# Four edits to a one-core encoder layer: one exponential per head over both key blocks, rotary tables on VectorE, late queries turned ahead of a round's last block, and an empty stage between load and squares

## The chip, the cores and the metric

The kernel runs on one NeuronCore of one Trainium2 chip, in one launch. A core has five engines with queues of their own: TensorE (PE, its weight loads shown as PEld), VectorE (DVE), ScalarE (ACT), GpSimd (POOL) and SyncE (SP), which here issues every DMA. The metric is the device time of the whole launch in microseconds, as the median of several runs.

## The reference: what is computed

One layer of a bidirectional encoder is applied to two groups of rows with the same weights: the prompt of 512 rows and the sample of 1024 rows, all of width 1024, in 32-bit floating point.

```python
a = _rmsnorm(h, norm_mix_g)
z = a @ w_in                                    # 1024 -> 8 q heads, 2 k, 2 v of 64, and 512 pooling channels
o_attn = _attention(q, k, v, q_norm_g, k_norm_g)  # q/k RMSNorm, 2-D rotary, softmax over all keys
o_pool = _pool_mixer(u, w_pool, pool_scale)       # means over windows of 2, 4, 8, 16, minus u, then 128x128
h = h + jnp.concatenate([o_attn, o_pool], axis=-1) @ w_out
m = _rmsnorm(h, norm_mlp_g)
h = h + jnp.square(jax.nn.relu(m @ w_up)) @ w_down   # 1024 -> 4096 -> 1024
gate = sigmoid(_rmsnorm(h, norm_ple_g) @ w_ple_gate)
h = h + gate * (p_i @ w_ple_proj)
return _rmsnorm(h, final_norm_g)
```

The softmax of a query row runs over 512 keys in the prompt and over 1024 keys in the sample.

## The kernel before

**Precision.** Each 32-bit operand of a large product is split into a high and a low part (`hi` a rounded copy, `lo` what is left), and a product is made of three matmuls (`three`, line 103). So nearly every operand passes two engines before TensorE can use it: a copy on ScalarE and a subtraction on VectorE or GpSimd.

**Order of the work.** The order on TensorE, ScalarE, VectorE and GpSimd is written out by hand: each engine runs its instructions in the order in which the code emits them, and waits for whatever the instruction at its head needs. Only SP's order, that of the DMAs, is found by the planner when the kernel is built. Most tiles in SBUF come from one pool of 49 buffers of the same size (`slot`, line 74); a load can be issued once a buffer is free for it. Two PSUM banks (`tp_ps`, line 84) serve all transposes and some small products in turn; a transpose waits until the bank it gets was read.

**The stages in order.**

1. *Input projection* (lines 1137 to 1183, to about 200 us). The rows are twelve tiles of 128: tiles 0 to 3 the prompt, 4 to 11 the sample. Tiles 0 and 1 run together while the weights arrive, then `mm_k(t, k)` goes tile by tile over eight slices `k`. `evac` (line 260) scales the result out of PSUM, squares the heads and sums them (VectorE, lines 280 and 282); `rstd_of` (line 97) makes the inverse root on GpSimd, an addition and a power (lines 99 and 100). `rotary_steps` (line 290) applies it and the rotary tables on VectorE (lines 292 to 309). One tile later `turn_qk` (line 327) transposes queries and keys into the two transposition banks as `qp` and `kp` and splits them (ScalarE lines 340 and 341, VectorE lines 343 and 344); `turn_u` (line 311) does the same for the pooling channels. The tables `tab` are the products of the gains with cosines and sines (lines 210 to 224); each is 128x512. GpSimd makes them, after a constant of ones (lines 201 to 203).
2. *Attention* (lines 1190 to 1285, to about 552 us). A `Unit` is a tile of 128 queries with one key/value head and its four query heads. The loop over `at` takes one query head per round: `soften` (the exponential of the head before, line 444), `score` (this head's scores and their maximum, line 433), `norm` (line 452), then `turn` and `split` (lines 463 and 470) of one or two key tiles of the unit before, and `weigh` (line 475), their product with the values. A round ends with one or two blocks out of `fill`: pieces of the pooling output or of the output projection (`pool_out`, `heads_out`), which are matmuls that need little from the other engines. In the prompt's rounds an even `at` takes two blocks and an odd one takes one; in the sample's rounds at most one is taken, and from `at` = 62 on only in some rounds. `extras` (line 1197) holds work that is left from the projection: `turn_u` of tile 11 in round 3, `turn_qk` of tile 10 in round 8 and of tile 11 in round 18, and the steps of the last rotary in rounds 6 to 10. It runs after the round's blocks (line 1270). GpSimd and ScalarE also run `chores`, a queue of generators that advance a step at a time, such as the preparation of the MLP's inputs (`make_m`, line 579).
3. *MLP* (from about 575 us). The rows are three chunks of 512. Products are arranged with seven instead of eight block products (`ORDER`, `UP`, `DOWN`); the prepared up-weights of the first chunk are kept in DRAM (`kept_d`) and fetched again for the others (tile `w`), and down-weights (`we`) are loaded and combined for pairs of tiles (`Double`). Between the products, `chores` finish the earlier chunks.
4. *Gate and final norm* (from about 1566 us): lines 1564 to 1630.

**The softmax.** For the sample a head's scores are 128x1024 over two PSUM banks, `S`. `soften` runs two exponentials, one for each block of 512 keys, each with its own accumulated sum; `norm` adds the two sums on VectorE (line 455), takes the reciprocal (line 456) and scales both blocks on GpSimd (line 461). A buffer of probabilities holds one key block of two heads. For the prompt there is one block, one sum and the reciprocal of line 458.

**The gating chore.** `gating(0)` (line 1394) runs during the third chunk's products. For each of four quarters of chunk 0 it loads the finished rows (`load_h` out of `hl_d`), squares them on ScalarE (line 1406) and scales them into the gate's inputs (lines 1357 and 1359), adds the squares on GpSimd (line 1413), and stores the inputs (line 1419). `staged` (line 667) interleaves the quarters: in a round, later stages of earlier quarters come ahead of earlier stages of later ones.

```python
    def staged(items, *stages):
        for t in range(len(items) + len(stages) - 1):
            for s in reversed(range(len(stages))):
                if 0 <= t - s < len(items):
                    yield from stages[s](items[t - s])
```

Of the kernel before, what the change touches and what calls it, by code (L numbers as in the profile page):

```python
# [18 lines left out]
P = 128  # L19
D = 1024  # L20
# [15 lines left out]
def encoder_layer(ctx, tc, xT, xn, xr, pT, w1, w2, w_pool, w_out, w_up, w_down, w_gate, w_proj,  # L36
# [18 lines left out]
    def load(dst, src):  # L55
        ins = sy.dma_start(dst, src).ins
        if last_pe[0] is not None:
            tc.add_manual_dep(ins, last_pe[0].name, NOSYNC, reason="not before its turn")
# [55 lines left out]
    def load_x(t, parts=(slice(0, KD),)):  # L114
        raw = slot([P, KD, P], F32, f"xt{t}")
        for part in parts:
            load(raw[:, part], xT[t][:, part])
        return raw
# [8 lines left out]
    def load_xn(t):  # L127
        nat = slot([P, D], F32, f"xn{t}")
        load(nat, xn[t * P:(t + 1) * P, :])
        return nat  # L130
# [34 lines left out]
    wps = tp_ps("warm")  # L165
    for i in range(8):
        pe.matmul(wps, wz[:, 0:P], wz, start=True, stop=True)
    load(gmix_sb, g_mix)
    head, tail = slice(0, 2), slice(2, KD)
    x0 = load_x(0, (head,))  # L170
# [13 lines left out]
    for k in range(3, KD):  # L184
        if k + 1 < KD:
            raws.append(load_w(k + 1))
        split_w(k, raws[k])
    n0, n1 = load_xn(0), load_xn(1)
    x2, n2 = load_x(2), load_xn(2)
    stat_x(0, n0)  # L190
    stat_x(1, n1)
# [6 lines left out]
    load(gmlp_sb, g_mlp)  # L198
    gfin_sb = const.tile([P, KD], F32, name="gfin_sb")
    load(gfin_sb, g_fin)  # L200
    ones_sb = const.tile([P, P], F32R, name="ones_sb")
    gp.memset(as32(ones_sb), 1.0)
    gp.tensor_scalar(ones_sb, as32(ones_sb), 1.0, 1.0, op0=ALU.mult, op1=ALU.mult)
    psc_sb = const.tile([P, 4], F32, name="psc_sb")
    load(psc_sb, p_scale)
    edge_sb = const.tile([P, 4, 2 * PAD], F32, name="edge_sb")
    load(edge_sb, edge)


    csr = slot([P, 2, 8, 32], F32, "csr")  # L210
    load(csr, cs)
    tab = {}
    for nm, g in (("q", q_g), ("k", k_g)):
        graw = small.tile([P, HD], F32, tag="graw", name=f"g{nm}", bufs=2)
        load(graw, g)
        if nm == "k":
            gp.tensor_scalar(graw, graw, 8.0, None, op0=ALU.mult)
        tb = slot([P, 2, 8, HD], F32, f"tab{nm}")
        for i in range(2):
            gp.tensor_tensor(  # L220
                tb[:, i].rearrange("p a (b c) -> p a b c", b=2),
                graw.rearrange("p (b c) -> p b c", b=2).unsqueeze(1).to_broadcast([P, 8, 2, 32]),
                csr[:, i].unsqueeze(2).to_broadcast([P, 8, 2, 32]), op=ALU.mult)
            tab[nm, i] = tb[:, i]

    def transpose4(dst, src):
        for i in range(4):
# [192 lines left out]
    class Unit:  # L420


        def __init__(self, s, t, g):
            self.s, self.t, self.g = s, t, g
            self.t0, self.n = SEQS[s]
            self.nc = self.n // 4
            self.id = f"{t}_{g}"
            self.sums = small.tile([P, 4, 2], F32, tag="sums", name=f"sums{self.id}", bufs=3)
            self.pr, self.S = {}, {}
            self.o = None  # L430
            self.pt = {}
# [11 lines left out]

        def soften(self, j):
            S, nm = self.S.pop(j)
            for c in range(self.nc):
                if j % 2 == 0:
                    self.pr[j // 2, c] = slot([P, 2, CH], F32, f"pr{self.id}{j}{c}")
                sc.activation(self.pr[j // 2, c][:, j % 2], S[:, c * CH:(c + 1) * CH], AF.Exp, bias=nm,
                              accum_out=self.sums[:, j, c:c + 1])  # L450

        def norm(self, j):
            rr = small.tile([P, 1], F32, tag="rr", name=f"rr{self.id}{j}")
            if self.nc == 2:
                ve.tensor_tensor(rr, self.sums[:, j, 0:1], self.sums[:, j, 1:2], op=ALU.add)
                ve.reciprocal(rr, rr)  # L456
            else:
                ve.reciprocal(rr, self.sums[:, j, 0:1])
            for c in range(self.nc):
                p = self.pr[j // 2, c][:, j % 2]  # L460
                gp.tensor_scalar(p, p, rr, 1.0, op0=ALU.mult, op1=ALU.mult)  # L461

        def turn(self, kt):
            tp = tp_ps(f"tp{self.id}{kt}")
            c, b = kt // 4, kt % 4
            for j in range(4):
                pe.transpose(tp[:, j * P:(j + 1) * P], self.pr[j // 2, c][:, j % 2, b * P:(b + 1) * P], id_sb)
            self.pt[kt] = tp

        def split(self, kt):  # L470
# [196 lines left out]
    def staged(items, *stages):  # L667
        for t in range(len(items) + len(stages) - 1):
            for s in reversed(range(len(stages))):
                if 0 <= t - s < len(items):  # L670
                    yield from stages[s](items[t - s])

    HALVES = (slice(0, CH), slice(CH, D))

# [543 lines left out]
    for at in range(2, 4 * len(units) + 6):  # L1218
# [41 lines left out]

        n = 0 if at < 3 else 2 - at % 2 if at < first_sample else 1
        took = n and bool(fill)
        for _ in range(n):
            if fill and (at < 62 or at % 2 == 0 and (at < 76 or at % 3 or len(fill) > 10) or at >= 96):
                fill.popleft()()
        fill.extend(ready)
        ready.clear()
        lag = fresh
        last = (cur, j) if cur else None
        if at in extras:  # L1270
            extras[at]()
        if at > 3:
            clock[0] += 1
            if products and products[0][0] < clock[0]:
# [119 lines left out]
    def gating(c):  # L1394
# [24 lines left out]
                sy.dma_start(hg_d[a][i], flat(gin[c, a][i]))  # L1419
            return iter(())  # L1420

        yield from staged(range(4), fetch, square, total, keep)
        gp.tensor_tensor(acc[:, 0], acc[:, 0], acc[:, 1], op=ALU.add)
        yield from wait(6)
        yield from spread_g(c, acc)
# [332 lines left out]
```

## Time and profile before

| what | value |
|---|---|
| median of 3 runs | 1769.13 us (1767.67 to 1769.21) |
| the profiled execution's own time | 1772.11 us |
| its span, first to last instruction | 1770.3 us |
| busy: PE, PEld | 1727.3 us, 1574.4 us |
| busy: DVE, ACT, POOL | 1287.1 us, 906.9 us, 1078.4 us |
| mean granted TensorE clock | 0.992 |
| moved by DMA | 391.78 MB, mean 221 GB/s |

Busy time is read per engine against the span; an engine far below it stands for most of the time and costs something only where another waits for it. In the timeline rows a line gives the start in us from the span's start, the length in us, the engine, the line of the kernel, the operation, the tiles written and read, the shape and the count; in brackets stands the idle time before it and what ended that. In rows of waits stand the total in us, the number of waits and the longest. In rows that group a line's instructions stand the count, then shortest, median and longest duration in ns. DMA rows give the count, the size of one and the median time from issue to landing in us.

### The profile page before, as it was taken

To read this page: it belongs to the slowest core of one execution; us is meant where nothing else is said; L and a number is where in the kernel's file an instruction comes from. 1 tells how busy PE (TensorE), PEld (TensorE's weight loads), DVE (VectorE), ACT (ScalarE), POOL (GpSimd) and SP (SyncE) were. 2 spreads that over 40 slices of the span, in tenths; PEclk is the share of its full clock that TensorE was granted. 3 is DMA by queue.
4 is the path that set the end of the run, shared out by engine and by line. 5 is a ranking of instruction groups with operands and counts; after the bars stand their busy time and mean duration, and the time that the engine had idled before them with its cause. 6 is when DMAs were issued, how large, how long until landed. Compare 5 with 4: busy or idle time off the path is not lost. (4 is left out here: it accounts for less than half of the span.)

```text
span 1770.3 us, 31419 instructions
## 1 busy us (share of the span) xinstructions
PE 1727.3 (98%) x11692; PEld 1574.4 (89%) x11692; DVE 1287.1 (73%) x1786; ACT 906.9 (51%) x1730; POOL 1078.4 (61%) x933
## 2 busy tenths in 40 slices
PE   9999999999999999999999999999999999999997
PEld 7788777888778998989989999999999999998897
DVE  5776765878987668777757766777778788675666
ACT  6334454767885646555445444544444445543333
POOL 3474883534765766859645776865678677654431
PEclk9999999999999999999999999999999999999998
DMA  7232544211326887979798969698776889653012
GB/s 253 84 133 106 217 175 179 72 67 42 124 92 256 322 296 274 361 277 357 285 348 324 344 226 334 223 340 331 248 265 233 308 276 349 252 208 114 12 48 96
DMA packets 133608, 391.78 MB, mean 221 GB/s; under 512 B 14160, under 2 KB 26832, under 8 KB 133456
## 3 DMA queue, kind: packets, MB, share of 16 engines
q1 hardware_dynamic: 133456, 389.78, 60.9%
q8 instruction: 92, 1.51, 0.4%
q14 instruction: 60, 0.49, 0.1%
HBM read 275.96 MB, written 113.77 MB: 220 GB/s over the span
## 5 line engine op out<-in xcount | busy, mean ns | idle before, releaser
L49 PE MATMUL pd<-ta,v 128*128 128x256 f32 x2688 | 339.4, 283 | 0.1
L49 PEld LDWEIGHTS pd<-ta,v 128*128 128x128 f32 x2688 | 329.6, 190 | 0.8 <-POOL v L1033 0.3
L1033 POOL TENSOR_TENSOR v<-we,v 128x512 fp32r<-128x512 f32 x128 | 184.4, 1461 | 105.7 <-DVE ta L1053 37.6
L461 POOL TENSOR_SCALAR pr<-pr,rr 128x512 f32<-128x512 f32 x160 | 111.2, 706 | 135.6 <-DVE rr L456 64.0
L49 PE MATMUL pd<-r,wd 128*128 128x512 f32 x768 | 190.5, 397 | 2.0 <-DVE r L950 2.0
L1033 POOL TENSOR_TENSOR v<-vs,v 128x512 fp32r<-128x512 f32 x96 | 128.0, 1354 | 103.6 <-DVE c L1056 37.2
L49 PE MATMUL z<-w,x 128*128 128x512 f32 (+1 forms) x864 | 175.0, 359 | 2.4 <-ACT w L159 1.1
L1053 DVE TENSOR_TENSOR ta<-c,ta 128x512 fp32r<-128x512 f32 x112 | 115.7, 1033 | 84.4 <-ACT ta L1051 77.1
L49 PEld LDWEIGHTS pd<-r,wd 128*128 128x128 f32 x768 | 140.9, 189 | 31.1 <-DVE r L950 2.8
L49 PEld LDWEIGHTS z<-w,x 128*128 128x128 f32 x864 | 142.4, 188 | 29.3 <-ACT w L159 2.8
L844 POOL TENSOR_TENSOR w<-ws,w 128x512 fp32r<-128x512 f32 x72 | 106.2, 1477 | 92.8 <-ACT w L843 88.0
L49 PE MATMUL pq<-mo,w 128*128 128x256 f32 x1152 | 153.2, 282 | 5.4 <-DMA w<-kept_d 4.2
L49 PE MATMUL pz<-mo,w 128*128 128x256 f32 x1152 | 153.6, 283 | 4.0 <-DVE u L980 3.5
L49 PE MATMUL px<-mo,w 128*128 128x256 f32 x1152 | 153.6, 283 | 0.0
L49 PEld LDWEIGHTS pz<-mo,w 128*128 128x128 f32 x1152 | 146.6, 190 | 7.7 <-DVE u L980 4.1
L49 PEld LDWEIGHTS pq<-mo,w 128*128 128x128 f32 x1152 | 143.7, 189 | 6.7 <-DVE H L1084 2.9
L49 PEld LDWEIGHTS px<-mo,w 128*128 128x128 f32 x1152 | 145.6, 191 | 1.4
L49 PE MATMUL pg<-hg,wg 128*128 128x512 f32 (+1 forms) x768 | 141.1, 338 | 0.3 <-DVE hg L1359 0.3
L49 PEld LDWEIGHTS pg<-hg,wg 128*128 128x128 f32 x768 | 119.3, 188 | 17.0 <-DVE hg L1359 0.5
L472 ACT CAST pt<-tp 128x512 fp32r<-128x512 f32 x160 | 87.7, 590 | 90.3 <-PE tp L53 88.6
L473 DVE TENSOR_TENSOR pt<-tp,pt 128x512 fp32r<-128x512 f32 x160 | 104.0, 684 | 31.4 <-ACT pt L472 31.0
L441 DVE TENSOR_REDUCE nm<-S 128x1 f32<-128x1024 f32 (+1 forms) x96 | 100.1, 1043 | 22.9 <-PE S L49 22.4
(252 smaller groups left out, 3562.2 us busy)
## 6 DMA issues: line engine op xcount, KB each, us to landing
w<-kept_d SPq DMA_DIRECT2D x210, 512.0 KB, 5.9
kept_d<-w SPq DMA_DIRECT2D x105, 512.0 KB, 5.2
we<-in_w_down_dram SPq DMA_DIRECT2D x64, 512.0 KB, 7.0
mo_d<-mm SPq DMA_DIRECT2D x84, 256.0 KB, 4.2
mo<-mo_d SPq DMA_DIRECT2D x42, 512.0 KB, 10.1
wur<-in_w_up_dram SPq DMA_DIRECT2D x36, 512.0 KB, 5.8
wdr<-in_w_down_dram SPq DMA_DIRECT2D x32, 512.0 KB, 6.8
h_d<-h SPq DMA_DIRECT2D x16, 512.0 KB, 2.9
```

The lines of the kernel that those rows point to most:

```text
L49: last_pe[0] = nc.tensor.matmul(*a, **k).ins
L441: ve.tensor_reduce(nm, S[:, :nch * CH], axis=AX.X, op=ALU.max, negate=True)
L461: gp.tensor_scalar(p, p, rr, 1.0, op0=ALU.mult, op1=ALU.mult)
L472: sc.copy(self.pt[kt][:, 0], tp)
L473: ve.tensor_tensor(self.pt[kt][:, 1], tp, as32(self.pt[kt][:, 0]), op=ALU.subtract)
L844: gp.tensor_tensor(t[:, 1], x, as32(t[:, 0]), op=ALU.subtract)
L1033: ins = gp.tensor_tensor(lo[:, p], src[:, p], as32(hi[:, p]), op=ALU.subtract).ins
L1053: last_ve[0] = ve.tensor_tensor(t[:, 1], x, as32(t[:, 0]), op=ALU.subtract).ins
```

## The change

The diff has four parts that do not touch each other's lines.

1. *Tables.* The load of the cosines and sines, the loads of the two gains and the four table products move ahead of the loads of tile 2 (`load_x(2)`, `load_xn(2)`) and run on VectorE instead of GpSimd. The constant of ones moves to the start of the kernel, behind the warm-up matmuls, and stays on GpSimd.
2. *Softmax.* A head's probabilities are one buffer of 1024 columns in the sample (in the prompt two heads share one); one exponential and one accumulated sum cover both key blocks, the addition of two sums is gone, and GpSimd scales both blocks in one instruction.
3. *Extras.* They run ahead of the round's last block instead of after it; in a round without blocks they run as before.
4. *Gating.* A stage that yields nothing stands between the load of a quarter and its squares, so that in `staged` each quarter's load is issued one turn earlier against its square.

```diff
+    ones_sb = const.tile([P, P], F32R, name="ones_sb")
+    gp.memset(as32(ones_sb), 1.0)
+    gp.tensor_scalar(ones_sb, as32(ones_sb), 1.0, 1.0, op0=ALU.mult, op1=ALU.mult)
     load(gmix_sb, g_mix)
...
     n0, n1 = load_xn(0), load_xn(1)
+    csr = slot([P, 2, 8, 32], F32, "csr")
+    load(csr, cs)
+    tab = {}
+    for nm, g in (("q", q_g), ("k", k_g)):
+        graw = small.tile([P, HD], F32, tag="graw", name=f"g{nm}", bufs=2)
+        load(graw, g)
+        if nm == "k":
+            ve.tensor_scalar(graw, graw, 8.0, None, op0=ALU.mult)
+        tb = slot([P, 2, 8, HD], F32, f"tab{nm}")
+        for i in range(2):
+            ve.tensor_tensor(
...
     x2, n2 = load_x(2), load_xn(2)
...
-    csr = slot([P, 2, 8, 32], F32, "csr")
...
-            gp.tensor_scalar(graw, graw, 8.0, None, op0=ALU.mult)
...
-            gp.tensor_tensor(
...
-            self.sums = small.tile([P, 4, 2], F32, tag="sums", name=f"sums{self.id}", bufs=3)
+            self.sums = small.tile([P, 4], F32, tag="sums", name=f"sums{self.id}", bufs=3)
...
         def soften(self, j):
             S, nm = self.S.pop(j)
-            for c in range(self.nc):
-                if j % 2 == 0:
-                    self.pr[j // 2, c] = slot([P, 2, CH], F32, f"pr{self.id}{j}{c}")
-                sc.activation(self.pr[j // 2, c][:, j % 2], S[:, c * CH:(c + 1) * CH], AF.Exp, bias=nm,
-                              accum_out=self.sums[:, j, c:c + 1])
+            n = self.nc * CH
+            if j not in self.pr:
+                full = slot([P, D], F32, f"pr{self.id}{j}")
+                for i in range(2 // self.nc):
+                    self.pr[j + i] = full[:, i * n:(i + 1) * n]
+            sc.activation(self.pr[j], S[:, :n], AF.Exp, bias=nm, accum_out=self.sums[:, j:j + 1])
 
         def norm(self, j):
             rr = small.tile([P, 1], F32, tag="rr", name=f"rr{self.id}{j}")
-            if self.nc == 2:
-                ve.tensor_tensor(rr, self.sums[:, j, 0:1], self.sums[:, j, 1:2], op=ALU.add)
-                ve.reciprocal(rr, rr)
-            else:
-                ve.reciprocal(rr, self.sums[:, j, 0:1])
-            for c in range(self.nc):
-                p = self.pr[j // 2, c][:, j % 2]
-                gp.tensor_scalar(p, p, rr, 1.0, op0=ALU.mult, op1=ALU.mult)
+            ve.reciprocal(rr, self.sums[:, j:j + 1])
+            p = self.pr[j]
+            gp.tensor_scalar(p, p, rr, 1.0, op0=ALU.mult, op1=ALU.mult)
...
+    def idle(item):
+        return iter(())
...
-        for _ in range(n):
-            if fill and (at < 62 or at % 2 == 0 and (at < 76 or at % 3 or len(fill) > 10) or at >= 96):
+        for i in range(max(n, 1)):
+            if i == n - 1 or not n:
+                extras.pop(at, lambda: None)()
+            if n and fill and (at < 62 or at % 2 == 0 and (at < 76 or at % 3 or len(fill) > 10) or at >= 96):
                 fill.popleft()()
...
-        if at in extras:
-            extras[at]()
...
-        yield from staged(range(4), fetch, square, total, keep)
+        yield from staged(range(4), fetch, idle, square, total, keep)
```

More of the change, by code (lines that the diff above doesn't have):

```diff
@@ L188, in encoder_layer @@
     n0, n1 = load_xn(0), load_xn(1)
+    csr = slot([P, 2, 8, 32], F32, "csr")
[9 more added lines that the diff above has]
+            ve.tensor_tensor(
+                tb[:, i].rearrange("p a (b c) -> p a b c", b=2),
+                graw.rearrange("p (b c) -> p b c", b=2).unsqueeze(1).to_broadcast([P, 8, 2, 32]),
+                csr[:, i].unsqueeze(2).to_broadcast([P, 8, 2, 32]), op=ALU.mult)
+            tab[nm, i] = tb[:, i]
     x2, n2 = load_x(2), load_xn(2)
@@ L200, in encoder_layer @@
     load(gfin_sb, g_fin)
-    ones_sb = const.tile([P, P], F32R, name="ones_sb")
-    gp.memset(as32(ones_sb), 1.0)
-    gp.tensor_scalar(ones_sb, as32(ones_sb), 1.0, 1.0, op0=ALU.mult, op1=ALU.mult)
     psc_sb = const.tile([P, 4], F32, name="psc_sb")
@@ L207, in encoder_layer @@
     load(edge_sb, edge)
-    csr = slot([P, 2, 8, 32], F32, "csr")
[L211 to L216, printed above, removed]
-            gp.tensor_scalar(graw, graw, 8.0, None, op0=ALU.mult)
[L218 to L224, printed above, removed]
     def transpose4(dst, src):
@@ L445, in soften @@
             S, nm = self.S.pop(j)
-            for c in range(self.nc):
-                if j % 2 == 0:
-                    self.pr[j // 2, c] = slot([P, 2, CH], F32, f"pr{self.id}{j}{c}")
-                sc.activation(self.pr[j // 2, c][:, j % 2], S[:, c * CH:(c + 1) * CH], AF.Exp, bias=nm,
-                              accum_out=self.sums[:, j, c:c + 1])
+            n = self.nc * CH
[4 more added lines that the diff above has]
+            sc.activation(self.pr[j], S[:, :n], AF.Exp, bias=nm, accum_out=self.sums[:, j:j + 1])
         def norm(self, j):
             rr = small.tile([P, 1], F32, tag="rr", name=f"rr{self.id}{j}")
-            if self.nc == 2:
-                ve.tensor_tensor(rr, self.sums[:, j, 0:1], self.sums[:, j, 1:2], op=ALU.add)
-                ve.reciprocal(rr, rr)
-            else:
-                ve.reciprocal(rr, self.sums[:, j, 0:1])
-            for c in range(self.nc):
-                p = self.pr[j // 2, c][:, j % 2]
-                gp.tensor_scalar(p, p, rr, 1.0, op0=ALU.mult, op1=ALU.mult)
+            ve.reciprocal(rr, self.sums[:, j:j + 1])
+            p = self.pr[j]
+            gp.tensor_scalar(p, p, rr, 1.0, op0=ALU.mult, op1=ALU.mult)
         def turn(self, kt):
             tp = tp_ps(f"tp{self.id}{kt}")
-            c, b = kt // 4, kt % 4
             for j in range(4):
-                pe.transpose(tp[:, j * P:(j + 1) * P], self.pr[j // 2, c][:, j % 2, b * P:(b + 1) * P], id_sb)
+                pe.transpose(tp[:, j * P:(j + 1) * P], self.pr[j][:, kt * P:(kt + 1) * P], id_sb)
             self.pt[kt] = tp
```

## The prediction

> **What bounds the kernel now.** I read the page first, then TensorE's own waits, then windows of 20 us and the timeline around each long wait.
>
> ```profile
> PE 1727.3 (98%) x11692; PEld 1574.4 (89%) x11692; DVE 1287.1 (73%) x1786; ACT 906.9 (51%) x1730; POOL 1078.4 (61%) x933
> ```
>
> TensorE is busy 1727.3 us of a span of 1770.3, and none of the edits removes a matmul. What the change can win is therefore only the 43.0 us in which TensorE stands, and what the clock loses behind a stand. The waits of TensorE (what waited, on what; us in total, times, longest) say where that is:
>
> ```profile
> PE pq L49 <- DMA w<-kept_d: 4.2, 3, 2.8
> PE qp L53 <- DVE eb L301: 4.1, 2, 2.5
> PE pz L49 <- DVE u L980: 3.5, 1, 3.5
> PE tp L53 <- DVE qs L343: 3.3, 2, 1.6
> PE o L49 <- DVE pt L473: 3.2, 7, 1.0
> ```
>
> Four of these five belong to the four edits: `qp` waits for the first rotary, which needs statistics that queue behind the tables on POOL; `pz` stands next to the gating loads; `tp` waits for banks that the late queries hold; `o` waits for the split of the turned probabilities in the sample's attention. Two stretches (us; busy us of PE, PEld, DVE, ACT, POOL; granted clock; DMA share) show what surrounds them:
>
> ```profile
> 440.00:560.00 120.00, 115.59 (x676) 91.34 (x676) 106.66 (x194) 100.59 (x239) 81.79 (x101) 1.00 0.34 123
> 1480.00:1500.00 20.00, 16.45 (x119) 16.24 (x118) 14.62 (x17) 8.19 (x13) 14.72 (x11) 0.83 0.86 326
> ```
>
> In the second half of the sample's attention TensorE is idle 120 - 115.59 = 4.4 us while VectorE and ScalarE are 89% and 84% busy: there the other engines set the pace now and then. Around 1490 us a stand of 3.5 us goes with a granted clock of 0.83.
>
> **Part 1: rotary tables on VectorE, ones earlier.**
>
> ```profile
> 22.68 0.33 SPq L56 DMA_DIRECT2D csr<-in_cs_dram  x1
> 32.35 1.23 DVE L125 TENSOR_TENSOR x<-xt,x 128x1024 fp32r<-128x1024 f32 x1 [3.60 <-ACT x L124]
> 33.71 2.54 POOL L220 TENSOR_TENSOR tabq<-gq,csr 128x512 f32<-128x512 f32 x2
> 36.98 0.82 DVE L282 TENSOR_REDUCE hs<-ra 128x10 f32<-128x640 f32 x1
> 37.28 2.54 POOL L220 TENSOR_TENSOR tabk<-gk,csr 128x512 f32<-128x512 f32 x2
> 41.67 1.99 POOL L100 TENSOR_TENSOR hr<-hr,mhalf 128x10 f32<-128x10 f32 x1
> 43.70 0.82 DVE L292 TENSOR_TENSOR ea<-ea,hr 128x640 f32<-128x640 f32 x1 [2.35 <-POOL hr L100]
> 44.55 0.69 DVE L295 TENSOR_TENSOR ra<-ea,tabq 128x512 f32<-128x512 f32 x1
> 46.52 0.41 DVE L301 TENSOR_TENSOR eb<-ra,ea 128x256 f32<-128x256 f32 x1
> 47.08 0.63 PE L53 MATMUL qp<-id_sb,eb 128*128 128x128 f32 x4 [2.49 <-DVE eb L301]
> 54.72 0.63 PE L53 MATMUL qp<-id_sb,eb 128*128 128x128 f32 x4 [1.58 <-DVE eb L301]
> xn<-in_xn_dram SPq DMA_DIRECT2D x12, 512.0 KB, 6.3
> ```
>
> The head sums of tile 0 are ready at 36.98 + 0.82 = 37.80, but POOL's last table ends at 37.28 + 2.54 = 39.82 and the power that VectorE needs only at 43.66. With the tables and the ones gone from POOL the power can follow the sums at once (some 0.4 us for the addition ahead of it), and `hr` is there near 40.2, 3.5 us sooner. VectorE then loses its idle 2.35 before L292, so the rotary ends 2.4 us or more earlier, and TensorE, which reached `qp` at 47.08 - 2.49 = 44.59, no longer waits. The second wait (1.58) follows the same chain one tile later: VectorE starts that rotary about 3 us earlier while TensorE comes 2.49 earlier; I leave 0.2 of it. Gain 2.49 + 1.4 = 3.9 us; bounds 2 and 4.1.
>
> What it adds: four products of 128x512 on VectorE, nearest row L295 with 0.69, so 2.8 us with the scaling of `gk`, 2.9. They stand in VectorE's order just ahead of L125, in whose front it idles 3.60 us: that is the cover. It holds if `csr` lands by 32.35 - 2.9 = 29.4. Its load is now issued ahead of tile 2's two loads instead of behind them, so before 22.68; a load of twice its size in this stage takes 6.3 us, which gives 29.0 at the latest. With the cover gone, L125 slips by what is missing, at most the 2.9. The two gain loads and `csr` pass the loads of tile 2 on SP's queue; 256 KB ahead of a 512 KB load delays that by half of its own time at worst, and only the casts of tile 2 stand behind it on ScalarE, which TensorE needs a tile later. I take nothing for it.
>
> A rule speaks against this part: the Trainium skill (GPSIMD Engine Reference, 8. Key points) says that GpSimd shares its SBUF interfaces with VectorE and contends with VectorE instructions that have two SBUF inputs, which the table products are. By that rule they would be slow only if POOL ran long operations beside them; POOL then has just the small statistics of two tiles, so that the sum is the same by rule and by rows.
>
> **Part 2: late queries ahead of the last block.**
>
> ```profile
> 220.85 3.04 PE L49 MATMUL pp<-yb,wo 128*128 128x512 f32 x12
> 222.94 0.66 DVE L473 TENSOR_TENSOR pt<-tp,pt 128x512 fp32r<-128x512 f32 x1
> 223.73 0.60 PE L53 MATMUL qp<-id_sb,eb 128*128 128x128 f32 x4
> 225.57 1.39 DVE L343 TENSOR_TENSOR qs<-qp,qs 64x512 fp32r<-64x512 f32 x2 [0.95 <-ACT qs L340]
> 227.10 0.63 PE L53 MATMUL tp<-id_sb,pr 128*128 128x128 f32 x4 [1.63 <-DVE qs L343]
> 267.16 0.63 PE L53 MATMUL tp<-id_sb,pr 128*128 128x128 f32 x4 [1.62 <-DVE qs L343]
> ```
>
> Two blocks (12 matmuls) take 223.73 - 220.85 = 2.88 us, one 1.44. Put behind the query's transposes instead of ahead, that block covers 1.44 us of the wait of 1.63. But the transposes need both banks, and the second comes free when L473 ends at 223.60; `qp`, now near 222.3, runs in the free bank, and `kp` waits some 0.7 to 0.9 us for the other. First place: gain 0.7. At the second place I expect 1.3, since there the split stands earlier against the blocks. The same move of `turn_u` in an early round hides some tenths. Together 2.2 us; bounds 0 (banks never free in time) and 3.3 + 0.3. The adds of the last block's output and the store of the queries only change places by one block.
>
> **Part 3: a stage between load and squares.**
>
> ```profile
> 1475.15 0.32 SPq L56 DMA_DIRECT2D h<-hl_d  x1
> 1481.71 1.06 ACT L1406 ACTIVATE sqg<-h 128x1024 f32<-128x1024 f32 x1 [3.35 <-DMA h<-hl_d]
> 1484.59 0.69 DVE L1053 TENSOR_TENSOR ta<-c,ta 128x512 fp32r<-128x512 f32 x1 [3.93 <-POOL sqg L1413]
> 1491.40 2.93 PE L49 MATMUL pz<-mo,w 128*128 128x256 f32 x12 [3.55 <-DVE u L980]
> 1498.19 1.58 PE L49 MATMUL pq<-mo,w 128*128 128x256 f32 x12
> SPq L56 <- POOL H L692: 5.7, 1, 5.7
> ```
>
> The load of the fourth quarter is issued at 1475.15, ScalarE's square stands 3.35 us for it, everything behind that in ScalarE's order (the casts that VectorE's L1053 reads) slips, VectorE idles 3.93, and TensorE stands 3.55 at 1487.85. The empty stage leaves every square where it is in the order and issues each load but the first one item earlier, ahead of the previous item's square and totals and of the stores of `hg`. No instruction is added. The square then runs 3.35 sooner, which takes 3.35 of the 3.55. The clock comes on top: 0.17 x 20 = 3.4 us of work lost in that window, seen as 12 matmuls in 2.93 instead of 1.58; part of the slow stretch lies inside the stand, so I take 2.3. Gain 5.6 us; bounds 0 and 3.55 + 3.4 = 6.9.
>
> The Trainium skill (TensorE: Matmul & The Clock Gate, Part 1) says that the window which decides on half speed is free-running. By that rule the clock's 2.3 belongs to how this stand happened to lie, and other stands that remain may catch or lose such a stretch after every shift; the sum would be 3.35 instead of 5.6 if one is caught anew.
>
> The cost is a buffer of 4 KB held longer, and the loads pass weights on SP's queue. The last row (of the waits of SP's queue from 1440 to 1500 us) is a load that stood 5.7 us until a buffer was released; behind it queue the kept weights `w` and the down weights `we`, which TensorE and POOL wait for.
>
> **Part 4: one exponential per head.**
>
> ```profile
> 446.43 0.71 ACT L449 ACTIVATE pr<-S,nm 128x512 f32<-128x512 f32 x1
> 447.10 0.71 ACT L449 ACTIVATE pr<-S,nm 128x512 f32<-128x512 f32 x1
> 448.50 1.30 POOL L610 TENSOR_TENSOR t<-m,t 128x512 f32<-128x512 f32 x1
> 448.54 1.27 DVE L455 TENSOR_TENSOR rr<-sums 128x1 f32<-128x1 f32 x1
> 450.67 1.25 PE L53 MATMUL tp<-id_sb,pr 128*128 128x128 f32 x8 [0.62 <-DVE pt L473]
> L455 DVE TENSOR_TENSOR rr<-sums x64: 145/151/1271, 317.7 to 551.1; 128x1 f32<-128x1 f32 x64
> L458 DVE RECIPROCAL rr<-sums x32: 147/154/164, 198.7 to 314.5; 128x1 f32<-128x1 f32 x32
> ```
>
> A 128x1024 exponential has no row: between 0.71 (width free) and 1.42 (twice), and the square of that shape took 1.06; with the pointer bias I take 1.12. The second half with its accumulator read costs 447.10 - 446.43 = 0.67 of pitch, the wider one 0.41, so ScalarE wins 0.26 a head, 64 x 0.26 = 17 us. VectorE loses 64 additions of two sums. Their median is 151 ns, but one lasted 1.27 us, and it ended at 449.81, just as POOL's subtraction did (449.80): the addition reads two SBUF operands, and it stood until POOL was done, with the split behind it and the transposes behind that (0.62). The reciprocal that stays never took over 164 ns in the prompt. POOL's scaling is one instruction instead of two, no dearer than both.
>
> None of this is on TensorE; it shows where TensorE waits for the split. Lower bound: 0.2 us less in each of the 7 waits for `o`, 1.4. Upper: the 4.4 idle of the window, and as much again in waits that modelled matmul ends hide, 9. I take 4.5, all of the visible idle: the addition and the exponential both stand ahead of the split. The probabilities of the first four key tiles keep their buffers two rounds longer; each head now takes its buffer only when it starts, so the number in use hardly changes.
>
> **Sum.** 3.9 + 2.2 + 5.6 + 4.5 = 16.2. The profiled execution took 1772.1 us (span 1770.3): 1755.9. It lies 3.0 above the median of 1769.1, so the median comes to 1752.9, said as 1753.
>
> **Rivals.**
>
> *Only the two long stands go.* The sample's attention stays bound by the loop transpose, cast, split, and `kp` pays in part 2 what `tp` wins. For it: most additions take 151 ns. Against: the quoted 0.62 follows a held one. Gain 3.9 + 5.6 = 9.5: 1760.
>
> *Attention gives its upper bound.* VectorE at 89% and ScalarE at 84% both become lighter, and short waits vanish too. 9 instead of 4.5, all else as summed: 1748.
>
> *No net change: the stand at 1488 moves.* The earlier loads of `h` meet a full set of buffers, the queue stands as in the row of 5.7, a kept weight comes late and TensorE stands 2.8 with the clock's loss behind it (2.3), twice; the attention gives its lower bound and part 2 nothing. 3.9 + 5.6 + 1.4 - 2 x 5.1 = 0.7: 1768.
>
> *Slower: the kept weights come late throughout.* SP has one order; when the moved loads and the other buffer pattern push `w` behind its use, each such place costs 2.8 + 2.3 = 5.1, as the worst wait for `kept_d` does now. From four places on (20.4) it outweighs the sum of 16.2: 1773. Against: 210 such loads show three waits today.
>
> **How the numbers follow.** Forecast 0.60, two long stands only 0.18, upper bound in attention 0.09, no net change 0.08, slower 0.05. Its own range is 1749 to 1758, from the bounds of parts 2 and 4. Up to 1746 and 1763 the two neighbours fall inside, with 0.13 outside. What this kernel's measurement can tell from no change is about 0.2%, 3.5 us: faster 0.87, same 0.08, slower 0.05.
>
> **What would show it.** Right: no wait of `qp` for L301 and L292 without idle time; L473 instead of L343 as what `tp` or `kp` waits for near 220 us; no DMA wait ahead of L1406, no wait of `pz` near 1490 and a clock of 1.00 there; L449 with about 1.12 us and no L455, and TensorE's idle time from 440 us to the end of attention at 1 us or less. Wrong: new waits of `pq` or `px` for `kept_d`, a wait of the matmuls `z` for tile 2's split, or the old idle time in attention with other names.

## The result, and the profile after

The changed kernel takes 1755.05 us (median of 4 runs, 1752.97 to 1756.67), the kernel before beside it 1769.17 us (4 runs, 1767.67 to 1770.17). The ratio is 0.992 with a 95% interval of 0.9903 to 0.9937: 14.1 us or 0.8% faster. The profiled execution of after took 1754.77 us, its span is 1753.0 us, 17.3 less than that of before; some 2 of these are a late start of that one execution, which is told below.

The page of after, engines; then the waits of TensorE (us in total, times, longest):

```profile
PE 1719.8 (98%) x11692; PEld 1570.6 (90%) x11692; DVE 1266.9 (72%) x1727; ACT 892.5 (51%) x1602; POOL 1059.0 (60%) x864
```

```profile
PE pq L49 <- DMA w<-kept_d: 4.3, 2, 2.2
...
PE pz L49 <- DVE u L977: 1.7, 2, 1.3
PE pq L49 <- DVE c L982: 1.1, 1, 1.1
PE qp L53 <- DVE eb L300: 1.0, 1, 1.0
```

The four waits that the edits were aimed at are smaller or gone: `qp` 4.1 to 1.0, `pz` 3.5 to 1.7 (but with 1.1 for `pq` from the same engine beside it), `tp` for the queries' split and `o` for the split of the probabilities are off the head of the list. The wait for `kept_d`, which the rivals feared for, is unchanged (4.2 to 4.3).

The same places in the timeline of after, in the order of the four parts (start, length, instruction, idle time before it and what ended that):

```profile
28.69 1.29 DVE L203 TENSOR_TENSOR tabq<-gq,csr 128x512 f32<-128x512 f32 x2 [0.76 <-DMA csr<-in_cs_dram]
31.34 1.22 DVE L125 TENSOR_TENSOR x<-xt,x 128x1024 fp32r<-128x1024 f32 x1
43.97 0.60 PE L53 MATMUL qp<-id_sb,eb 128*128 128x128 f32 x4
45.87 1.39 DVE L342 TENSOR_TENSOR qs<-qp,qs 64x512 fp32r<-64x512 f32 x2 [1.15 <-ACT qs L339]
50.43 0.42 DVE L300 TENSOR_TENSOR eb<-ra,ea 128x256 f32<-128x256 f32 x1
51.00 0.63 PE L53 MATMUL qp<-id_sb,eb 128*128 128x128 f32 x4 [0.98 <-DVE eb L300]
219.94 0.44 PE L53 MATMUL kp<-id_sb,ea 128*128 128x128 f32 x2 [0.75 <-DVE pt L467]
261.09 0.63 PE L53 MATMUL tp<-id_sb,pr 128*128 128x128 f32 x4 [0.56 <-DVE qs L342]
```

The first `qp` no longer waits, the second does. The late query's `kp` waits 0.75 us for a bank; the second place keeps 0.56 us of 1.62.

Windows of after (us; busy us of PE, PEld, DVE, ACT, POOL; granted clock, DMA share, GB/s): the last 120 us of attention, the stretch around the gating loads, and one further on where nothing was edited:

```profile
428.00:548.00 120.00, 118.49 (x704) 95.61 (x703) 97.78 (x169) 97.97 (x183) 77.70 (x71) 1.00 0.35 126
1463.00:1483.00 20.00, 17.60 (x146) 17.19 (x144) 17.62 (x19) 8.69 (x15) 17.82 (x11) 1.00 0.99 367
...
1340.00:1360.00 20.00, 17.87 (x138) 17.70 (x138) 14.97 (x15) 7.17 (x12) 17.90 (x13) 0.91 0.62 212
```

In attention TensorE stands 1.5 us instead of 4.4. Near 1475 us the clock is full where it was 0.83, but TensorE still stands for 2.4 us. And near 1350 us there is now a clock of 0.91; before has 1.00 at this place (1357 to 1377 us there), and so has a second trace of the changed kernel (1340 to 1360 us):

```profile
1357.00:1377.00 20.00, 18.92 (x160) 18.74 (x159) 15.23 (x15) 8.43 (x14) 17.61 (x13) 1.00 0.63 222
```

### The profile page after: what moved, and what is told of

Its sections match the earlier page's. It is cut to its first block, busy times and chain, and to the rows that moved or that the text cites. A ratio compares the mean times of both kernels' runs of the same rounds, so it can differ in the third digit from the quotient of the medians.

```text
span 1753.0 us, 31242 instructions
## 1 busy us (share of the span) xinstructions
PE 1719.8 (98%) x11692; PEld 1570.6 (90%) x11692; DVE 1266.9 (72%) x1727; ACT 892.5 (51%) x1602; POOL 1059.0 (60%) x864
## 5 line engine op out<-in xcount | busy, mean ns | idle before, releaser
L456 POOL TENSOR_SCALAR pr<-pr,rr 128x1024 f32<-128x1024 f32 (+1 forms) x96 | 95.4, 994 | 140.8 <-DVE rr L454 73.9
```

## Each part alone

The first four runs put one part each into the kernel before, everything else as it was.

```diff
 tables alone
+            ve.tensor_tensor(
+                tb[:, i].rearrange("p a (b c) -> p a b c", b=2),
...
     x2, n2 = load_x(2), load_xn(2)
 extras alone
+            if i == n - 1 or not n:
+                extras.pop(at, lambda: None)()
...
-        if at in extras:
-            extras[at]()
 idle alone
-        yield from staged(range(4), fetch, square, total, keep)
+        yield from staged(range(4), fetch, idle, square, total, keep)
 exp alone
+            sc.activation(self.pr[j], S[:, :n], AF.Exp, bias=nm, accum_out=self.sums[:, j:j + 1])
...
-                ve.tensor_tensor(rr, self.sums[:, j, 0:1], self.sums[:, j, 1:2], op=ALU.add)
```

> The kernel before with the rotary tables made on VectorE ahead of tile 2's loads, and the ones earlier, alone. Theory (the waits of qp are the gain, and the second one stays because the loop rotary, copy, split, rotary takes 7.03 us against 6.05 us of TensorE's work): 3.3 us faster than before, with one wait of qp for L301's addition of 0.9 to 1.1 us and none at the first place. Rival 1 (the prediction's own term): 3.9 us, second wait 0.2. Rival 2 (the half-speed stretches of the clock are what was won): the gain is 3.3 plus or minus multiples of 1.7 us according to how many half-speed stretches of 3.4 us the profile shows against five of them before.

> The kernel before with the extras run ahead of a round's last block, alone. Theory: 2.0 to 2.4 us faster; kp waits 0.7 to 0.9 us at the first place, near 222 us, tp 0.3 to 0.6 us at the second, near 267 us. Rival 1 (banks are never free in time): 0 to 0.5 us. Rival 2 (both waits gone): 3.3 us.

> The kernel before with the empty stage in gating, alone. Theory after the result (the wait of the squares for the load was only the first of several causes; behind it VectorE is held beside GpSimd's two-input additions and ScalarE waits for a buffer): the stand of 3.55 us becomes stands of 2 to 2.5 us together in the stretch from 1470 to 1495 us, without the half-speed stretch of 6.8 us, so that 1.2 to 1.5 us come from the stand and 2.3 to 3.4 us from the clock, 3.5 to 5 us in all. Rival 1 (the prediction): 5.6 us, stands of 0.2 us. Rival 2 (the stands that remain come from the other edits): stands of 0.2 us here although the kernel after shows 2.4.

> The kernel before with one exponential per head, alone. Theory: 6.4 us faster, as between the two traces from 267 to 551 us, with TensorE's idle time in the 120 us ahead of the end of attention at 1.5 us instead of 4.4. Rival 1 (the prediction's term): 4.5 us. Rival 2 (only seven visible waits shorten): 1.4 us. If the four parts run alone give 3.3 + 2.2 + 4 + 6.4 = 15.9 us, they add up to the 14.1 us of the whole change within their intervals; a sum that is well above it says that parts win the same time twice or that the clock's half-speed stretches fall anew with each shift.

| part alone | ratio to before (95%) | gain in us (of 1768.1) | mean granted clock (before 0.9946) |
|---|---|---|---|
| tables | 0.9990 (0.9978 to 1.0003) | 1.8 (-0.5 to 3.9) | 0.9944 |
| extras | 0.9977 (0.9964 to 0.9990) | 4.1 (1.8 to 6.4) | 0.9953 |
| idle | 0.9984 (0.9972 to 0.9996) | 2.8 (0.7 to 5.0) | 0.9959 |
| exp | 0.9969 (0.9955 to 0.9983) | 5.5 (3.0 to 8.0) | 0.9943 |

The sum is 14.2 us. The changed kernel, run once more for the comparisons below, gives 0.9924 (0.9911 to 0.9936), 13.4 us, so within the intervals the parts add up; none is seen to win the time of another. Ahead of the runs 3.3, 2.0 to 2.4, 3.5 to 5 and 6.4 us were expected. Tables and idle came lower, though their intervals still reach these values.

> The changed kernel once more, unaltered, as the one that the three others of this stage are compared with. Theory (the gains of the four parts run alone, 1.5, 3.7, 3.1 and 6.0 us as means, add up): 13 to 15 us faster than the kernel before. Rival (parts win the same time twice): 10 to 12 us.

**The clock's share.** 70 runs of the kernel before list granted clocks from 0.991 to 0.998, and their times go with them: 20 runs at 0.994 average 1769.8 us, 9 runs at 0.996 average 1765.1. A straight line fitted to all runs of this study, with a level of its own for each kernel, gives 1.25 us for 0.001 of clock. The nine runs of the changed kernel average 0.9966 against 0.9946, which by that line is 2.5 us of its gain. The same line takes 1.7 us of clock out of the idle part's gain and 1.0 out of the extras', and leaves 1.5, 2.6, 1.3 and 6.3 us for tables, extras, idle and exp (each plus or minus 0.9). So the half-speed stretches explain a part, as a rival had it, but the parts differ after they are taken out. The line is only a fit: it does not say whether the clock or the stand came first.

**Tables.** The wait of 2.49 us that the prediction removed was that one execution's. Three of the kernels just run make the tables as before; the timelines of exp alone and idle alone in turn:

```profile
29.79 1.22 DVE L125 TENSOR_TENSOR x<-xt,x 128x1024 fp32r<-128x1024 f32 x1 [2.52 <-ACT x L124]
29.52 0.20 POOL L202 MEMSET ones_sb<- 128x128 f32 x1
44.58 0.63 PE L53 MATMUL qp<-id_sb,eb 128*128 128x128 f32 x4 [1.34 <-DVE eb L301]
52.23 0.63 PE L53 MATMUL qp<-id_sb,eb 128*128 128x128 f32 x4 [1.58 <-DVE eb L301]
```

```profile
30.32 0.20 POOL L202 MEMSET ones_sb<- 128x128 f32 x1
45.51 0.63 PE L53 MATMUL qp<-id_sb,eb 128*128 128x128 f32 x4 [1.74 <-DVE eb L301]
52.56 0.63 PE L53 MATMUL qp<-id_sb,eb 128*128 128x128 f32 x4 [0.98 <-DVE eb L301]
```

Extras alone has waits of 1.33 and 0.99 us, and a fourth kernel with the old tables (the scalar form below) 1.74 and 0.98. So the first wait is 1.3 to 1.7 us there, the second `qp` starts between 52.23 and 53.45, and the profiled before had 54.72. In eight traces with the tables edit and the old place of the rotary it starts between 50.17 and 52.99, at 51.4 on average. That is 1.3 us earlier than in the four, or 1.7 with the profiled before, which is the size of the measured gain. The other 2 us between the two first traces came from a late start of one of them, whose ones were made at

```profile
32.05 0.21 POOL L202 MEMSET ones_sb<- 128x128 f32 x1
```

The second wait comes in two sizes, 1.58 us in before and exp alone, 0.98 to 1.00 in the others. In those two the subtraction L125 behind the first rotary lasts 2.31 us and GpSimd's L1150 (`wp`; L1145 in exp alone) beside it 1.41 and 1.42; in idle alone, extras alone, the scalar form, tables alone and after L125 lasts 1.21 to 1.22 and the `wp` 2.55 to 2.56. In each trace one of the two is long and the other short. In all traces with the tables edit the second wait is 0.98 to 1.00 us (0.89 with the moved rotary below), so the edit wins these 0.6 us where the old kernel loses them, and about 1 us stays.

**Extras.** The waits of the run alone are those of after, 0.76 and 0.53 us (the rows of its `kp` and `tp`), so 1.63 + 1.62 - 0.76 - 0.53 = 2.0 us are shown. From the second `qp` to the last `o` of attention (start to start) exp alone takes 504.65 us and the changed kernel 502.49, at full clock in both: 2.2 us for the extras. What the runs gave beyond that, 2.6 without the clock, is within their intervals.

```profile
221.47 0.44 PE L53 MATMUL kp<-id_sb,ea 128*128 128x128 f32 x2 [0.76 <-DVE pt L473]
...
262.60 0.63 PE L53 MATMUL tp<-id_sb,pr 128*128 128x128 f32 x4 [0.53 <-DVE qs L343]
```

**Idle.** Alone it leaves the same two stands as after (waits of TensorE from 1465 to 1495 us), so they do not come from the other edits. One stand of 3.55 us became 2.5 us: the stand gave 1.0, the clock the rest. The traces show the sum: from a `px` (at 1453.51 us in before, 1439.52 in after) to the first `pg` of the gate, 114.94 to 117.75 us pass in the five kernels without the empty stage (before, the other three parts alone and the scalar form below), 116.1 on average, and 113.13 here, so 3.0 us are won.

```profile
PE pz L49 <- DVE u L983: 1.4, 1, 1.4
PE pq L49 <- DVE c L988: 1.1, 1, 1.1
```

## The second wait of the tables

```diff
-            if k == 3:
+            if k == (2 if t == 2 else 3):
                 rotary(t - 1)
```

> The changed kernel with tile 1's rotary issued on VectorE ahead of the split of tile 0's queries instead of behind it. Theory (the second wait of qp, 0.98 us, comes from the loop qp of tile 0, its copies and split, then tile 1's rotary, 7.03 us, and VectorE's 1.39 us of split in it are what is too much): the second wait of qp is gone and the time is 0.9 to 1.0 us below that of the changed kernel in this stage; the first wait may come back by some tenths if the power of tile 1 is not there yet. Rival (VectorE is not what sets it; the power of tile 1 or TensorE's own order is): the wait keeps 0.7 to 1.0 us, or goes to the two waits for tile 0's split.

The ratio is 0.9934 (0.9921 to 0.9946), 11.7 us under before against 13.4 for the changed kernel: not faster. The timeline shows why:

```profile
48.17 0.42 DVE L300 TENSOR_TENSOR eb<-ra,ea 128x256 f32<-128x256 f32 x1
49.01 1.39 DVE L342 TENSOR_TENSOR qs<-qp,qs 64x512 fp32r<-64x512 f32 x2
50.55 0.63 PE L53 MATMUL qp<-id_sb,eb 128*128 128x128 f32 x4 [0.89 <-DVE qs L342]
```

The rotary is done at 48.59, but now the split of tile 0 is late, and with it the bank that `qp` needs: 0.89 instead of 0.98. Both lie on VectorE between the two `qp`, and whichever is last is waited for. The rival was right: another order moves this wait and does not remove it.

## What the one exponential won

Two runs take its two halves apart. In one the changed kernel gets a VectorE addition ahead of the reciprocal back (the sum plus a column of zeros); in the other the kernel before keeps both exponentials and only its addition changes form, from two tensors to one tensor and a per-partition scalar.

```diff
+                ve.tensor_tensor(rr, self.sums[:, j:j + 1], mzero[:, 0:1], op=ALU.add)
+                ve.reciprocal(rr, rr)
```

```diff
-                ve.tensor_tensor(rr, self.sums[:, j, 0:1], self.sums[:, j, 1:2], op=ALU.add)
+                ve.tensor_scalar(rr, self.sums[:, j, 0:1], self.sums[:, j, 1:2], None, op0=ALU.add)
```

> The changed kernel, but in the sample a VectorE addition of the single sum and a column of zeros, of 128x1 with two operands in SBUF, stands ahead of the reciprocal again, so that the one exponential is left alone as a gain. Theory (the addition that is now and then held beside GpSimd gave most of the 6 us): the attention is 3 to 5 us slower than in the changed kernel, with TensorE's idle time in the 120 us before the end of attention at 3.5 to 4.5 us instead of 1.5. Rival (ScalarE's shorter exponential gave most of it): 0 to 1.5 us slower, idle 1.5 to 2.5 us.

> The kernel before with only the addition of the two sums changed: the second sum is given as a per-partition scalar instead of as a second tensor; the two exponentials stay. Theory (what holds the addition beside GpSimd is its second tensor operand in SBUF): no addition over 0.2 us, TensorE's idle time in the last 120 us of attention falls from 4.4 to 1.5 to 2.5 us, and 4 to 5.5 us are won on the kernel before. Rival 1 (any VectorE instruction with two SBUF sources of any kind is held, or the place in the order is what matters): additions of over 1 us stay and the time is that of before within 1 us. Rival 2 (the shorter exponential is needed as well): 2 to 3 us.

With the addition back the ratio to before is 0.9953 (0.9940 to 0.9965): 8.3 us, 5.1 less than the changed kernel of the same stage. With the scalar form alone, before becomes 0.9980 (0.9969 to 0.9991), 3.5 us (1.6 to 5.5) faster. The additions by count, shortest, median and longest in ns, first with the addition back, then in the scalar form:

```profile
L457 DVE TENSOR_TENSOR rr<-sums,mzero x64: 144/150/1042, 311.0 to 542.7; 128x1 f32<-128x1 f32 x64
```

```profile
L455 DVE TENSOR_SCALAR rr<-sums x64: 200/205/215, 316.5 to 546.3; 128x1 f32<-128x1 f32 x64
```

The scalar form is 54 ns dearer in the median and never held. Windows of 120 us at the end of attention, in the same order:

```profile
428.00:548.00 120.00, 116.34 (x680) 92.30 (x679) 105.80 (x197) 96.03 (x181) 77.31 (x69) 1.00 0.32 113
```

```profile
440.00:560.00 120.00, 117.73 (x705) 95.00 (x704) 101.16 (x197) 101.01 (x240) 83.52 (x100) 1.00 0.39 138
```

TensorE stands 3.7 us with a held addition and the short exponential, 2.3 us without a held addition and with both exponentials, 1.5 in the changed kernel and 4.4 in before. So the held addition was the larger cause: the rest of the edit is worth 5.5 - 3.5 = 2.0 us without a held addition and only 5.5 - 5.1 = 0.4 beside one, both with intervals of some 3 us. The traces measure it closer. From the last `qp` to the last `o` of attention (start to start, at full clock) 302.15 us pass in before, 298.13 in the scalar form and 295.52 in exp alone; with the extras moved 302.39 in extras alone, 300.78 with the addition back and 296.09 in after. So 4.0 of 6.6 us, or 4.7 of 6.3, go with the addition, and 2.6 or 1.6 with the rest. That rest is not ScalarE's alone: GpSimd's scaling, too, is one instruction instead of two (1.13 us on average where two took 2 x 0.71), and in the 2.6 the addition's own 0.2 us goes as well. No run takes these apart. That the exponential alone gave most of it, the rival, is out.

The Trainium skill (SBUF — State Buffer, section SBUF: two separate sides) states that VectorE and GpSimd share a pair of ports, which a VectorE instruction with two SBUF inputs and a GpSimd instruction that reads SBUF take from each other for the whole length of an instruction. The traces agree: 1271 ns in before (151 in the median), and 200 to 215 for the form with one tensor; that a per-partition scalar out of SBUF does not count as the second input is what the run adds.

## The stands that remain in the gating stretch

VectorE's order in after from 1467 us on, GpSimd's beside it, and ScalarE's one wait there:

```profile
1467.41 1.68 DVE L1050 TENSOR_TENSOR ta<-c,ta 128x512 fp32r<-128x512 f32 x1 [0.94 <-ACT ta L1048]
1469.01 2.31 DVE L1035 TENSOR_TENSOR vs<-we,vs 128x1024 f32<-128x1024 f32 x1
1471.24 1.78 DVE L1356 SCALAR_TENSOR_TENSOR hg<-h,gple_sb,hg 128x512 fp32r<-128x512 f32 x1
1472.95 1.21 DVE L1081 TENSOR_TENSOR H2u<-pd,H2u 128x1024 f32<-128x1024 f32 x1
1474.08 0.74 DVE L1356 SCALAR_TENSOR_TENSOR hg<-h,gple_sb,hg 128x512 fp32r<-128x512 f32 x1
1474.74 0.41 DVE L977 TENSOR_TENSOR u<-pz,u 128x256 f32<-128x256 f32 x1
1475.08 1.96 DVE L1027 TENSOR_TENSOR we<-we,we 128x1024 f32<-128x1024 f32 x1
1476.96 1.78 DVE L1050 TENSOR_TENSOR ta<-c,ta 128x512 fp32r<-128x512 f32 x1
...
1467.26 2.98 POOL L1410 TENSOR_TENSOR sqg<-sqg,sqg 128x512 f32<-128x512 f32 x2
1470.20 3.97 POOL L1030 TENSOR_TENSOR v<-we,v 128x512 fp32r<-128x512 f32 x2
1474.14 4.05 POOL L1410 TENSOR_TENSOR sqg<-sqg,sqg 128x512 f32<-128x512 f32 x2
...
1470.27 0.39 ACT L971 ACTIVATE c<-px 128x256 f32<-128x256 f32 x1 [1.94 <-POOL sqg L1410]
```

Behind the load that the prediction removed stood VectorE itself: no gap from 1467.41 to 1481.14, and the additions `u` and `c` that TensorE's banks wait for (L977, L982) come at their place in that row (L982 at 1480.40, two instructions behind the last one shown). The trace of before had this to show already: behind the load's wait VectorE works without a gap from 1484.59 to 1496.2 there, with two scalings that take far more than the 0.74 us of the shortest:

```profile
1486.34 1.78 DVE L1359 SCALAR_TENSOR_TENSOR hg<-h,gple_sb,hg 128x512 fp32r<-128x512 f32 x1
...
1489.17 1.84 DVE L1359 SCALAR_TENSOR_TENSOR hg<-h,gple_sb,hg 128x512 fp32r<-128x512 f32 x1
```

Four runs ask what fills VectorE's order in after: the additions of squares moved to VectorE; left out; and spread by more turns in two strengths (two turns behind each half, as below; then `wait(1 + e)` there and `wait(4)` ahead of the sum). The first two lines are one edit, the others another.

```diff
-                    gp.tensor_tensor(acc[:, e], acc[:, e], sqs[a][:, e], op=ALU.add)
+                    ve.tensor_tensor(acc[:, e], acc[:, e], sqs[a][:, e], op=ALU.add)
...
-                yield
+                yield from wait(2)
...
-        yield from wait(6)
+        yield from wait(2)
```

> The changed kernel with the six additions of gating's squares (128x512, two operands in SBUF) on VectorE instead of GpSimd. Theory (the 1.31 and 1.09 us that TensorE still stands near 1474 and 1480 us come from VectorE's scaling and subtractions that are held beside these additions): both stands fall below 0.5 us together and the time is 1.5 to 2.3 us less, although VectorE gets 6 x 0.7 = 4.2 us of work. Rival (VectorE's own work sets the pace there): the stands stay or grow to 3 to 4 us, and the time is the same or 1 to 2 us more.

> The changed kernel without the six additions of gating's squares: the squares of the second, third and fourth quarter are computed but not added, so that the gate's mean square of chunk 0 leaves out three quarters of the columns. Theory (VectorE's order from 1467 to 1480 us has no gap, and its two-input instructions there last up to 1.1 us longer than alone because GpSimd works beside them without a pause; the additions make that pause vanish): the stands of 1.31 and 1.09 us near 1474 and 1480 us fall below 0.3 us together, ScalarE's wait of 1.94 us for a buffer of squares is gone, and the time is 2 to 2.5 us below the 1754.9 us of the changed kernel. Rival (VectorE's own work sets the pace, as the additions on VectorE suggest, where the stand grew to 3.79 us): a stand of 0.8 to 2 us stays, and 0 to 1.2 us are won.

> The changed kernel with two turns instead of one behind each half of gating's totals, and two turns instead of six ahead of the sum over rows: the additions lie further apart, nothing is added or left out. Theory (GpSimd works without a pause from 1463.9 to 1478.2 us, and this is what slows VectorE there): the two stands, 2.4 us together, fall to 0 to 0.8 us, and 1.5 to 2.4 us are won on the changed kernel's 1754.9 us. Rival (the same pairs meet elsewhere, or buffers are held longer and a kept weight comes late): stands of 2 us or more in other places, 0 or a loss of up to 3 us.

> The changed kernel with one turn more behind the second half only of each of gating's totals, and four turns instead of six ahead of the sum over rows: half the spreading of the run before, two turns behind the changed kernel at the end instead of four. Theory (spreading helps the two stands near 1474 and 1480 us, and its loss came from the sum that TensorE then met too early, 2.31 us with a slow clock behind it): the two stands fall below 1 us together, the sum is met without a wait, the stand of 1.05 us near 1553 us stays away, and 1 to 2 us are won on the changed kernel's 1754.9 us. Rival (GpSimd's work is only moved and meets TensorE's later products in any case): other stands of 1.5 us or more between 1480 and 1560 us, and 0 to 3 us lost.

| kernel | ratio to before (95%) | gain in us | TensorE's waits of 0.5 us and more, 1465 to 1560 us |
|---|---|---|---|
| changed kernel | 0.9924 (0.9911 to 0.9936) | 13.4 | 1.31 and 1.08 for VectorE |
| additions on VectorE | 0.9942 (0.9929 to 0.9956) | 10.3 | 3.79 for VectorE |
| without the additions | 0.9917 (0.9900 to 0.9934) | 14.7 | none |
| spread by two | 0.9953 (0.9938 to 0.9967) | 8.3 | 2.31 for the sum, 1.05 for a weight's low part |
| spread by one | 0.9928 (0.9915 to 0.9942) | 12.7 | 1.59 and 1.26 for `u` of the next pair, 0.63 for the low part |

Without the additions the stretch is free of waits, and the same instructions are short again:

```profile
1466.98 0.94 DVE L1050 TENSOR_TENSOR ta<-c,ta 128x512 fp32r<-128x512 f32 x1 [0.43 <-ACT ta L1048]
1467.85 1.21 DVE L1035 TENSOR_TENSOR vs<-we,vs 128x1024 f32<-128x1024 f32 x1
...
1472.82 1.21 DVE L1027 TENSOR_TENSOR we<-we,we 128x1024 f32<-128x1024 f32 x1
1473.95 0.68 DVE L1050 TENSOR_TENSOR ta<-c,ta 128x512 fp32r<-128x512 f32 x1
```

(2.31 - 1.21) + (1.96 - 1.21) + (1.78 - 0.68) + (1.68 - 0.94) = 3.7 us of VectorE's 13 in this stretch go when these additions go. In the kernel's time the 2.4 us of stands are not seen to come back, since the intervals of 13.4 and 14.7 us overlap. The trace shows it for the stretch: from that `px` to the first `pg` 110.22 us pass without the additions, against 113.13 to 113.19 in five traces that have the empty stage and the additions as in the changed kernel. With VectorE doing the additions itself TensorE's wait grows, with a slow clock behind it:

```profile
1479.11 2.40 PE L49 MATMUL pz<-mo,w 128*128 128x256 f32 x12 [3.79 <-DVE u L977]
```

Spreading takes the two stands away, as the theory said, and makes others. In the stronger form TensorE meets the sum before GpSimd has it (first row); in the weaker one it waits twice for ScalarE's copy `u` of a next pair (second row). In both GpSimd brings one low part late (1.05 and 0.63 us).

```profile
1498.69 1.51 PE L49 MATMUL ssg<-ones_sb,sqg 128*128 128x1 f32 x8 [2.31 <-POOL sqg L1420]
```

```profile
1486.57 1.68 PE L49 MATMUL px<-mo,w 128*128 128x256 f32 x12 [1.59 <-ACT u L962]
```

No version of these is measurably faster than the changed kernel.

## Why the prediction was right, and where it was not

The forecast was 1753.0 us; 1755.05 came, inside the range, and the forecast's case: all four edits gain, each by the wait that was named, though for the tables the interval just takes in zero. The sum was 16.2 us against 14.1 measured. That it came so close is partly luck: tables and empty stage were 4.9 us too high together, late queries and exponential 2.9 too low. The two first traces differ by 17.3 us: 3.7 up to the second `qp`, 8.7 from there to the last `o` of attention, 1.6 in the MLP up to the `px` named above (before has one half-speed stretch more there), 3.2 from there to the first `pg`, and 0.2 after it.

- **Tables: 3.9 forecast, 1.8 (-0.5 to 3.9) measured.** Two steps failed. The first wait of 2.49 was taken from one execution, in which GpSimd made its ones 0.9 to 2.5 us later than in four others; their waits are 1.3 to 1.7. And "I leave 0.2 of it" for the second wait: it keeps 0.98. The prediction compared starts (VectorE 3 us, TensorE 2.49 earlier), but the second `qp` depends on the first: copies, split and tile 1's rotary take from 43.97 to 51.00, 7.03 us, and TensorE stands for the last 0.98 of them, whenever the first `qp` starts. The cover held against the profiled execution (`csr` used from 28.69, where 29.4 was allowed; L125 at 31.34 instead of 32.35), not against others (29.79 with the tables on GpSimd), but no wait of `z` for tile 2's split followed.
- **Late queries: 2.2 forecast, 4.1 (1.8 to 6.4) measured**, 2.6 without the clock. `kp`'s wait of "some 0.7 to 0.9" for the second bank was 0.75. At the second place 0.56 stayed where 0.3 was left. The 2.2 us that two traces give for the whole stretch are the forecast's term.
- **Empty stage: 5.6 forecast, 2.8 (0.7 to 5.0) measured.** The step that failed is "The square then runs 3.35 sooner, which takes 3.35 of the 3.55". The load's wait is gone, but the next in line, VectorE held beside GpSimd's additions and working without a gap, left 2.4 of the 3.55, and before's own rows of 1.78 and 1.84 us pointed to it. The clock's 2.3 was about right: 1.7 by the runs.
- **One exponential: 4.5 forecast, 5.5 (3.0 to 8.0) measured.** The exponential's 1.12 us was met (1.13 in the row below), and the idle time left in attention is 1.5 us where "1 us or less" was named. The mechanism, an addition that GpSimd's subtraction holds, carries most of it; the text's 17 us of ScalarE carry at most the smaller part. The term was set by the idle time of the last 120 us. Over the whole stretch from the last `qp` to the last `o` the traces give 6.6 us, of which 3.7 are less idle time of TensorE (7.85 to 4.11) and 2.9 shorter busy time (294.30 to 291.41), which the text had only in its upper bound.

```profile
L450 ACT ACTIVATE pr<-S,nm 128x1024 f32<-128x1024 f32 x64 | 72.1, 1127 | 0.4
```

- **The clock.** From the free-running window that the Trainium skill states (TensorE: Matmul & The Clock Gate, Part 1) the prediction worked out that stretches may come and go with every shift. The traces agree in part. One of 0.91 near 1350 has come, and the second trace of the changed kernel has none there but one of 0.91 from 1060 to 1080 us. The one near 1490, though, hangs on the stand: the five traces without the empty stage have stands of 3.0 to 4.9 us for `u` and a clock of 0.83 to 0.92 between 1480 and 1500 us, all of them; the seven with the empty stage and stands of at most 1.6 us in this place have 1.00, all of them; and where the additions on VectorE brought back a stand of 3.79 us, the clock was 0.92 again. So the clock's term hung on the stand, and only its size varied (0.83 in three of the five traces, 0.91 and 0.92 in two). In the mean of many runs the changed kernel has the higher clock, 0.9966 against 0.9946.
- **The rivals.** A kept weight that comes late did not happen (4.2 and 4.3 us). "Only the two long stands go" had the attention's small waits as worthless; they were the largest term.
- **Signs and range.** Two of the signs named did not come: `qp` still waits 0.98 us for what was L301, and TensorE's idle time at the end of attention is 1.5 us. The range of 1749 to 1758 does not quite follow from its bounds: with 3.6 and 9 for parts 2 and 4 the sum is 22.1, which gives 1747.

## What to carry to other kernels

A stand read from one profiled execution near the start of a kernel can be that execution's own: profile a second time before a term is made of it. Ahead of a wait that is to be removed, look what would end last next, by following the other engines' orders through the same stretch without a gap; here it was two thirds of the stand, and the rows of before showed it. And a tiny VectorE instruction with two SBUF tensors on a path beside busy GpSimd is worth removing, or giving the scalar form, even where its median says 0.15 us.

## What was not expected of the hardware

- A per-partition scalar operand keeps an addition of 128x1 at 200 to 215 ns beside GpSimd, where two tensors made it 145 to 1271 (mean 322 against a median of 151, so 64 x 0.17 = 11 us of VectorE in all):

```profile
L455 DVE TENSOR_TENSOR rr<-sums 128x1 f32<-128x1 f32 x64 | 20.6, 322 | 2.0 <-ACT pr L449 2.0
```

- The clock drops beside a stand of 2.13 us (window of 0.91 above; the row below), and stays full around two stands of 1.31 and 1.09 six us apart. In the 14 traces, from 60 us to the gate, all 14 stands of 2.7 us and more (2.72 to 4.85) have a half-speed stretch beside them, while of the stands between 1.7 and 2.7 us some do (1.75, 2.13, 2.37) and some do not (2.12, 2.47, 2.64). One and the same kernel differs by several us with its clock: before averages 1772.5 us in 2 runs at 0.991 and 1765.0 in 4 runs at 0.997.

```profile
1355.17 1.98 PE L49 MATMUL pq<-mo,w 128*128 128x256 f32 x12 [2.13 <-DMA w<-kept_d]
```
